# Delta recurrence: the second head of each pair contracts on the other 64 partitions, with exchanged copies of its k and qk products

## The chip, the cores and the metric

The kernel runs on one core of a Trainium2 chip. The metric is device time in microseconds (us); lower is better. Engines are named as the profile names them: PE (TensorE matmuls), PEld (TensorE weight loads), DVE (VectorE), ACT (ScalarE), POOL (GpSimd), SP (SyncE, which here issues most DMAs).

## The reference, cut to what matters

One decoder layer in fp32: a half-step feed-forward block, a combined projection, then two groups of eight heads side by side (dilated-window attention and a gated delta rule), an output projection, and a second half-step feed-forward block. 512 prompt tokens run beside 32 sample tokens (8 sequences of 4) that also read a key and value cache. The change touches the delta rule of the prompt. It goes in chunks of 64 tokens; the state `s` is 64x64 for each head and is carried from chunk to chunk:

```python
kd = k * exp(gc[..., -1:] - gc)               # k with decays
intra = tril(q @ k^T * decay)                # inside one chunk, 64x64 a head
...
def step(s, xs):
    v_new = u_i - w_i @ s
    o_i = qd_i @ s + intra_i @ v_new
    s = s * gl_i + kd_i^T @ v_new
    return s, o_i
```

So every chunk and head needs four products of 64x64 by 64x64: two with the state, then two with `v_new`. The last two, `kd_i^T @ v_new` and `intra_i @ v_new`, are the ones that the change makes in another way.

## The kernel before, in words

Dense products (both feed-forward blocks, the projections) are fp32 made of three passes over split operands, so each appears as `bank<-g,wh` twice and `bank<-g,wl` once. All of PE's products go through one helper and so bear one line, L309. One fp32 product of 64x64 shows as two MATMUL records of 64x64; a group of 16 records is 8 products.

The middle of the program (combined projection, delta rule, attention) is not written in the order in which it runs. It is written as lanes: Python generators that yield the engine, the planned microseconds and the PSUM banks of each next step. A planner, `Weave`, takes the step with the earliest planned start, and so sets the order of every engine's queue. A lane that needs buffers of the `g` pool yields ("G", n), and stands still until the planner's count of free slots allows it; ("G", -n) gives slots back. The pool has 63 buffers, of which the planner starts with `SLOTS - 23`. The lanes that matter here:

- `gemms()` makes the combined projection unit by unit (dense work, marked "PE*"); for the later units it asks for one slot before the first half of a unit. After light products the planner prefers dense ones that are ready.
- `weights()` casts the projection's weights on ACT (L921) and subtracts the high part on DVE (L923).
- `pair(j)` makes, for two heads (a pair, `hp` 0 and 1), the k-k and q-k products and writes IN[j] (the `intra` of both heads); `scale(j)` scales k to KD[j] on POOL; `inverse()` and `solve(j)` make the triangular inverse and the u and w operands. `solve` already uses two diagonal quarters of the PE array for pairs (`bank<-vu,wf`).
- `recurrence()` runs 8 steps, chunk after chunk. Step i = 2u + p2 has its 64 tokens on partitions r (the lower half where p2 is 0, the upper where it is 1); `ro` is the other half. One step: 16 products with the state (`bank<-state,wf` and `bank<-state,g`), a POOL multiply of the state (L1469), two DVE subtractions that make `v_new` in vv (L1474), 8 products into bank pk, KD with vv (L1481), and a DVE add that makes the new state (L1483).
- `chunk_out()`, one lane for each step, makes 8 products into bank pi, IN with vv (L1499), two DVE multiplies (L1502) and a DVE add of 64x512 (L1506). After each second step it makes the norm: an ACT square (L1511), a DVE reduction (L1514), some 13 small DVE operations (L1516 to L1520, helper lines 494 to 506), a POOL multiply (L1524), four PE transposes (L1529) and eight DVE multiplies (L1534).
- the attention's lanes: workers (L1731, L1746, L1812), the key cache (issued by SP at L1860, transposed by PE at L1866) and the value cache. The key loads need `g` slots; 15 of them come free when the recurrence ends.

In chunk_out and recurrence of before both heads of a pair read vv on the same partitions:

```python
mm(pk[64*hp:64*hp+64, j*64:j*64+64], KD[j][r, c0:c0+64], vv[r, j, hp])              # L1481
mm(pi[ro, (2*j+hp)*64:(2*j+hp)*64+64], IN[j][r, c0:c0+64], vv[r, j, hp])            # L1499
```

For pk the two heads of a pair use the same rows of the array (r) and different columns; for pi they use the same rows and the same columns (ro).

## Time and profile before

| | |
|---|---|
| median of the runs | 1219.39 us (3 runs, 1216.69 to 1222.22) |
| the profiled execution | 1218.54 us, of which the span is 1216.8 us |
| mean granted TensorE clock | 0.977 of full speed |
| PE busy | 1167.1 us, 96% of the span |
| DVE / ACT / POOL busy | 905.4 / 515.8 / 288.0 us |
| the eight recurrence steps | 600 to 667 us |

A row of the timeline gives the start, the length, the engine, the line and the form of a run of like instructions; ends of PE rows are modelled and overlap the next row, so the pitch from one row's start to the next is the better measure of what a group costs PE. In square brackets stands the idle time before a row and what ended it. Granted clock 1.00 is 2.4 GHz, the half of it is 1.2 GHz.

### The profile page before, as it was taken

How to read it: one execution, taken by the hardware profiler on the slowest of the kernel's cores; microseconds unless marked ns; L12 is line 12 of the kernel's file. 1: busy time of each engine (PE TensorE's matmuls, PEld its weight loads, DVE VectorE, ACT ScalarE, POOL GpSimd, SP SyncE). 2: the span in 40 equal slices, each digit the busy share in tenths (PEclk: the TensorE clock that was granted, in tenths of full speed). 3: DMA queues.
4: the chain of work that ended last, by engine and by line, in shares of the span. 5: the costliest groups of instructions: out<-in, count | busy, mean ns of one | idle time of the engine just before them, and what ended most of it. 6: DMA issues, size and time to landing. Idle time of an engine off the chain costs nothing.

```text
span 1216.8 us, 25657 instructions
## 1 busy us (share of the span) xinstructions
PE 1167.1 (96%) x10375; PEld 1104.9 (91%) x10375; DVE 905.4 (74%) x1905; ACT 515.8 (42%) x1035; POOL 288.0 (24%) x363
## 2 busy tenths in 40 slices
PE   8899999999999999999999999988999999999994
PEld 7899999999999888999888675877999999999994
DVE  6878887877766587794366647688988777777767
ACT  6444444343444465433411544456444444444432
POOL 2321121111100047961314100033211111111003
PEclk8999999999999999999999999989999999999997
DMA  7553323322233222336104995321322324242112
GB/s 169 152 174 97 115 88 108 105 73 87 70 97 121 75 69 78 97 91 159 58 13 124 322 299 191 114 77 46 113 92 73 98 79 122 87 122 70 56 50 74
DMA packets 165442, 130.91 MB, mean 108 GB/s; under 512 B 31758, under 2 KB 152100, under 8 KB 165324
## 3 DMA queue, kind: packets, MB, share of 16 engines
q1 hardware_dynamic: 163852, 124.82, 34.3%
q0 software_dynamic: 1472, 4.46, 1.2%
q8 instruction: 81, 1.33, 0.5%
q14 instruction: 37, 0.30, 0.1%
HBM read 119.63 MB, written 12.33 MB: 108 GB/s over the span
## 4 chain that ended last, share of the span: by engine, by line
PE 77%; DVE 10%; DMA 4%; POOL 3%; ACT 2%; SPq 2%; issue 2%; DVEq 0%; POOLq 0%; ACTq 0%
PE bank L309 73%; PE bank L525 1%; PE bank L1866 1%; DVE wl L313 1%; DMA wf<-in_ffn_w_gate 1%; DMA wf<-in_ffn_w_up 1%; DMA g<-in_cache_attn_k 1%; PE bank L582 1%; DVE wf L1333 1%; PE bank L1812 1%; DVE tmp L1331 1%; DVE wl L923 1%; DVE lna L504 1%; DVE g L313 1%; DVE g L1001 1%
## 5 line engine op out<-in xcount | busy, mean ns | idle before, releaser
L309 PE MATMUL bank<-g,wh 128*128 128x272 f32 (+2 forms) x4864 | 943.5, 292 | 11.9 <-DVE g L313 7.0
L309 PEld LDWEIGHTS bank<-g,wh 128*128 128x128 f32 x4864 | 769.4, 190 | 24.5 <-DVE g L313 7.6
L309 PE MATMUL bank<-g,wl 128*128 128x272 f32 (+2 forms) x2432 | 703.6, 290 | 0.0
L309 PEld LDWEIGHTS bank<-g,wl 128*128 128x128 f32 x2432 | 460.8, 190 | 3.6 <-issue 3.2
L312 ACT CAST wh<-wf 128x512 fp32r<-128x512 f32 (+2 forms) x176 | 111.7, 648 | 138.8 <-PE bank L309 113.0
L712 POOL TENSOR_TENSOR wf<-wf 128x512 f32<-128x512 f32 x40 | 63.7, 1592 | 360.5 <-DVE vu L710 344.9
L313 DVE TENSOR_TENSOR wl<-wf,wh 128x512 fp32r<-128x512 f32 (+2 forms) x172 | 135.6, 799 | 11.1 <-ACT wh L312 9.0
L309 PE MATMUL bank<-g 64*64 64x64 f32 (+15 forms) x1708 | 128.7, 295 | 3.7 <-DVE g L1596 2.4
L309 PEld LDWEIGHTS bank<-g 64*64 64x64 f32 (+7 forms) x1708 | 89.8, 142 | 23.2 <-issue 10.7
L312 ACT CAST wh<-vu 128x512 fp32r<-128x512 f32 x120 | 72.3, 618 | 70.7 <-PE bank L309 70.0
L713 POOL TENSOR_TENSOR vu<-wf,vu 128x512 f32<-128x512 f32 x40 | 59.7, 1493 | 125.4 <-DVE wl L313 121.1
L313 DVE TENSOR_TENSOR wl<-vu,wh 128x512 fp32r<-128x512 f32 x120 | 81.5, 693 | 10.4 <-ACT wh L312 6.2
L313 DVE TENSOR_TENSOR g<-g 128x544 fp32r<-128x544 f32 (+1 forms) x80 | 71.4, 919 | 0.0
L312 ACT CAST wh<-g 128x512 fp32r<-128x512 f32 x64 | 38.0, 618 | 59.5 <-issue 42.0
L312 ACT CAST g<-g 128x544 fp32r<-128x544 f32 (+1 forms) x80 | 44.3, 582 | 39.6 <-DVE g L755 24.0
L313 DVE TENSOR_TENSOR wl<-g,wh 128x512 fp32r<-128x512 f32 x64 | 43.0, 693 | 24.2 <-ACT wh L312 23.4
L887 ACT COPY g<-bank 128x512 f32<-128x512 f32 (+4 forms) x64 | 30.3, 501 | 60.0 <-PE bank L309 21.6
L923 DVE TENSOR_TENSOR wl<-wf,wh 128x1024 fp32r<-128x1024 f32 x28 | 37.7, 1348 | 20.6 <-ACT wh L921 20.4
L775 DVE TENSOR_TENSOR g<-bank,g 128x272 f32<-128x272 f32 x96 | 40.0, 431 | 12.5 <-PE bank L309 12.4
L711 DVE TENSOR_TENSOR vu<-vu,wf 128x512 f32<-128x512 f32 x40 | 47.6, 1190 | 1.8
L710 DVE TENSOR_TENSOR vu<-wf 128x512 f32<-128x512 f32 x40 | 27.5, 689 | 20.9 <-DMA wf<-in_ffn_w_gate 18.3
L921 ACT CAST wh<-wf 128x1024 fp32r<-128x1024 f32 x28 | 29.2, 1050 | 28.0 <-PE bank L309 14.0
(313 smaller groups left out, 1116.7 us busy)
## 6 DMA issues: line engine op xcount, KB each, us to landing
wf<-in_ffn_w_gate SPq DMA_DIRECT2D x21, 1024.0 KB
wf<-in_ffn_w_up SPq DMA_DIRECT2D x21, 1024.0 KB
g<-in_ffn_w_down SPq DMA_DIRECT2D x64, 256.0 KB
wf<-in_w_in SPq DMA_DIRECT2D x14, 1024.0 KB
g<-in_cache_attn_k SPq DMA_DIRECT2D x32, 256.0 KB
g<-in_cache_attn_v SPq DMA_DIRECT2D x32, 256.0 KB
wf<-in_ffn_w_down SPq DMA_DIRECT2D x8, 768.0 KB
wf<-in_w_out SPq DMA_DIRECT2D x4, 1024.0 KB
```

The lines of the kernel that those rows point to most:

```text
L309: return PE.matmul(out, l, r, start=start, stop=stop, skip_group_check=again)
L312: S.copy(h, f)
L313: (GP if pool else V).tensor_tensor(l, f, h.bitcast(F32), op=ALU.subtract)
L504: V.tensor_mul(a, y, y)
L710: V.tensor_add(s1, a21, a22)
L711: V.tensor_sub(s2, s1, a11)
L712: GP.tensor_tensor(a21, a11, a21, op=ALU.subtract)
L713: GP.tensor_tensor(s4, a12, s2, op=ALU.subtract)
L775: V.tensor_add(r, pd, r)
L887: return S.copy(out, src)
L921: S.copy(h, fm)
L923: V.tensor_sub(l, fm, h.bitcast(F32))
```

## The change

For the second head of each pair (hp 1), vv is written to the other half of the partitions (ro), and its KD and IN are read from copies in which the two halves of the partitions are exchanged (KX, IX). So the two heads of a pair contract on different rows of the array. `exchange()` makes the copies on ACT: two instructions of 64x256 for each of four pairs and each of KD and IN, 16 in all. They live in four more `g` buffers, taken one by one in `pair` (before its DMAs are issued) and at the end of `scale`, and given back when the recurrence ends (-19 where -15 was). The products into pi now land on ro for hp 0 and on r for hp 1, so the final add (one 64x512) becomes two of 64x256. The planned PE time of the pk and pi steps goes from 0.7 to 0.45, that of the add from 0.65 to 0.75.

```diff
@@ -1200,6 +1200,23 @@
         yield "G", -1
 
     EM, SD = {}, {}
+    KX, IX = {}, {}
+    def exchange(to, j, src):
+        if j % 2 == 0:
+            to[j // 2] = G(512)
+        x = to[j // 2][:, j % 2 * 256:j % 2 * 256 + 256].rearrange("p (u c) -> p u c", u=4)
+        for p2 in range(2):
+            S.copy(x[64 - 64 * p2:128 - 64 * p2], v4(src)[64 * p2:64 * p2 + 64, :, 1])
+
+    def chunk_of(own, exchanged, j, hp, u, p2):
+        if hp:
+            return exchanged[j // 2][64 - 64 * p2:128 - 64 * p2, j % 2 * 256 + u * 64:j % 2 * 256 + u * 64 + 64]
+        return own[j][64 * p2:64 * p2 + 64, u * 128:u * 128 + 64]
     A21 = [G(512) for _ in range(2)]
     svd = dp.tile([2, 2, 4, 4, 2, 32, 32], F32, name="svd")
     xd = dp.tile([2, 2, 4, 4, 2, 32, 32], F32, name="xd")
@@ -1260,6 +1277,10 @@
             yield "DVE", 0.35, [pa[hp]]
             V.tensor_tensor(v4(it)[:, :, hp], pv[hp][:, 1], v4(em)[:, :, hp], op=ALU.mult)
         IN[j] = it
+        if j % 2 == 0:
+            yield "G", 1
+        yield "ACT", 0.6
+        exchange(IX, j, it)
         av = at.rearrange("p (n c) -> p n c", n=8)
         for p2 in range(2):
             for hf in range(2):
@@ -1311,6 +1332,10 @@
             yield "POOL", 1.05
             x = VU[:, j] if c == 8 else a[j]
             GP.tensor_tensor(v4(x if out is None else out[j]), v4(x), b64(b[:, :, hs]), op=ALU.mult)
+        if j % 2 == 0:
+            yield "G", 1
+        yield "ACT", 0.6
+        exchange(KX, j, KD[j])
         wv.post(("scaled", j))
 
     def inverse():
@@ -1471,14 +1496,13 @@
                 vv = vn.rearrange("p (j t e) -> p j t e", j=4, t=2)
                 yield "DVE", 0.7
                 for hp in range(2):
-                    V.tensor_tensor(vv[r, :, hp], VU[r, :, u * 128 + hp * 64:u * 128 + hp * 64 + 64], pb[hp][r, :256].rearrange("p (j e) -> p j e", j=4),
+                    V.tensor_tensor(vv[(r, ro)[hp], :, hp], VU[r, :, u * 128 + hp * 64:u * 128 + hp * 64 + 64], pb[hp][r, :256].rearrange("p (j e) -> p j e", j=4),
                                     op=ALU.subtract)
-                yield "PE", 0.7, 2
+                yield "PE", 0.45, 2
                 pk, pi = wv.bank(), wv.bank()
                 for j in range(4):
                     for hp in range(2):
-                        c0 = u * 128 + hp * 64
-                        mm(pk[64 * hp:64 * hp + 64, j * 64:j * 64 + 64], KD[j][r, c0:c0 + 64], vv[r, j, hp])
+                        mm(pk[64 * hp:64 * hp + 64, j * 64:j * 64 + 64], chunk_of(KD, KX, j, hp, u, p2), vv[(r, ro)[hp], j, hp])
                 yield "DVE", 0.35, [pk]
                 V.tensor_tensor(sn, pk[:, :256].rearrange("p (j e) -> p j e", j=4), sn, op=ALU.add)
                 ST = sn
@@ -1486,24 +1510,25 @@
         for hp in range(2):
             GP.dma_start(sg_p[0, 0].rearrange("(j t) d e -> t d j e", t=2)[hp], ST[64 * hp:64 * hp + 64])
         yield "T", 6.0
-        yield "G", -15
+        yield "G", -19
 
     def chunk_out(u, p2, vv, pb, pi, ov):
         r = slice(64 * p2, 64 * p2 + 64)
         ro = slice(64 - 64 * p2, 128 - 64 * p2)
         ou = ov.rearrange("p j t e -> p (j t e)")
-        yield "PE", 0.7
+        yield "PE", 0.45
         for j in range(4):
             for hp in range(2):
-                c0 = u * 128 + hp * 64
-                mm(pi[ro, (2 * j + hp) * 64:(2 * j + hp) * 64 + 64], IN[j][r, c0:c0 + 64], vv[r, j, hp])
+                mm(pi[(ro, r)[hp], (2 * j + hp) * 64:(2 * j + hp) * 64 + 64], chunk_of(IN, IX, j, hp, u, p2), vv[(r, ro)[hp], j, hp])
         for hp in range(2):
             yield "DVE", 0.35, [pb[hp]]
             V.tensor_tensor(ov[ro, :, hp], pb[hp][ro, :256].rearrange("p (j e) -> p j e", j=4),
                             egs[ro, u, :].rearrange("p (j t) -> p j t", t=2)[:, :, hp, None].to_broadcast([64, 4, 64]),
                             op=ALU.mult)
-        yield "DVE", 0.65, [pi]
-        V.tensor_tensor(ou[ro], pi[ro], ou[ro], op=ALU.add)
+        yield "DVE", 0.75, [pi]
+        pv = pi.rearrange("p (j t e) -> p j t e", j=4, t=2)
+        for hp in range(2):
+            V.tensor_tensor(ov[ro, :, hp], pv[(ro, r)[hp], :, hp], ov[ro, :, hp], op=ALU.add)
         if p2 == 0:
             return
         yield "ACT", 0.55
```

The planner works out every engine's order from the planned times and the free slots, so the four more slots and the new planned times move work that the diff does not name. Three places:

PE of before, in the fifth recurrence step: the state products, dense products (`g,wh`, `g,wl`) that the planner put behind them, and then one group of eight products with vv.

```order
L309 MATMUL bank<-state,wf_7088 64x64 x4
L309 MATMUL bank<-state,g 64x64 x2
L309 MATMUL bank<-state,wf_7088 64x64 x4
L309 MATMUL bank<-state,g 64x64 x6
L309 MATMUL bank<-g,wh 128x256 x2
L309 MATMUL bank<-g,wl 128x256
L309 MATMUL bank<-g,wh 128x256 x2
L309 MATMUL bank<-g,wl 128x256
L309 MATMUL bank<-g 64x64 x16
```

PE of the changed kernel, the fifth and sixth steps, from the group with vv of the step before; L1554 are the transposes of the norm (L1529 before).

```order
L309 MATMUL bank<-g 64x64 x16
L309 MATMUL bank<-state,wf_7117 64x64 x8
L309 MATMUL bank<-state,g 64x64 x8
L309 MATMUL bank<-g 64x64 x16
L309 MATMUL bank<-state,wf_7117 64x64 x8
L309 MATMUL bank<-state,g 64x64 x8
L309 MATMUL bank<-g 64x64 x16
L1554 MATMUL bank<-cst,g 128x128 x4
L309 MATMUL bank<-g 64x64 x16
L309 MATMUL bank<-g,wh 128x256 x2
L309 MATMUL bank<-g,wl 128x256
```

The dense products that stood between the state products and the products with vv are gone from these two steps; from the fifth step to the eighth 24 dense matmuls stand where 110 stood, and the rest comes behind the recurrence, beside the first key transposes (L1866 before, L1891 now).

DVE of before, from the end of the fourth step into the fifth: small operations of a norm, the multiplies L1534 of the norm before, the subtractions L1474, the multiplies L1502, an evacuation (L888) and the new state (L1483).

```order
L505 SCALAR_TENSOR_TENSOR da<-da,oss 128x8
L1534 TENSOR_TENSOR g<-bank,g 128x64 x8
L506 SCALAR_TENSOR_TENSOR dy<-da,dy 128x8
L1474 TENSOR_TENSOR g<-vu,bank 64x4x64 x2
L1502 TENSOR_TENSOR g<-bank,egs 64x4x64 x2
L504 TENSOR_TENSOR da<-dy 128x8
L888 COPY g<-bank 128x512
L505 SCALAR_TENSOR_TENSOR da<-da,oss 128x8
L1483 TENSOR_TENSOR state<-bank,state 128x256
L506 SCALAR_TENSOR_TENSOR orr<-da,dy 128x8
L1506 TENSOR_TENSOR g<-bank,g 64x512
```

DVE of the changed kernel at the same place; L1499, L1525, L1507, L1531, L1539 and L1559 are L1474, L1502, L1483, L1506, L1514 and L1534 of before.

```order
L1499 TENSOR_TENSOR g<-vu,bank 64x4x64
L1525 TENSOR_TENSOR g<-bank,egs 64x4x64
L1499 TENSOR_TENSOR g<-vu,bank 64x4x64
L1525 TENSOR_TENSOR g<-bank,egs 64x4x64
L1559 TENSOR_TENSOR g<-bank,g 128x64 x8
L1507 TENSOR_TENSOR state<-bank,state 128x256
L1531 TENSOR_TENSOR g<-bank,g 64x4x64 x2
L1539 TENSOR_REDUCE oss<-g 128x8
L1499 TENSOR_TENSOR g<-vu,bank 64x4x64 x2
L1525 TENSOR_TENSOR g<-bank,egs 64x4x64 x2
L1541 TENSOR_TENSOR oss<-oss,rq_4909 128x8
L1542 TENSOR_SCALAR oss<-oss 128x8
```

Each add of chunk_out is two instructions now, and the eight multiplies of the norm and its reduction stand between one state and the next subtraction.

ACT of before, in the stretch that prepares the pairs: weight casts (L921), evacuations of the projection (L989, L991), squares (L1225, L1283) and the convolution's activation (L998).

```order
L921 CAST wh<-wf_5654 128x1024
L1225 ACTIVATE g<-g 128x512
L989 COPY g<-bank 128x256
L991 COPY g<-bank 128x32
L998 ACTIVATE g<-g,cw 128x512
L989 COPY g<-bank 128x256
L1283 ACTIVATE g<-g 128x512
L989 COPY g<-bank 128x256
L991 COPY g<-bank 128x32
```

ACT of the changed kernel at the same place, with the exchanging copies (L1213).

```order
L921 CAST wh<-wf_5654 128x1024
L989 COPY g<-bank 128x256
L991 COPY g<-bank 128x32
L1242 ACTIVATE g<-g 128x512
L1213 COPY g<-g 64x256 x2
L998 ACTIVATE g<-g,cw 128x512
L1213 COPY g<-g 64x256 x4
L989 COPY g<-bank 128x256
L1213 COPY g<-g 64x256 x2
L989 COPY g<-bank 128x256
```

Eight of the sixteen copies stand between the evacuations of the projection here.

## Rows read from the trace of the kernel before

**Rows 1.** Chain that ended last, 540 to 700 us: start us, us, what.
```profile
611.58 17.91 PE bank L309 x259
629.49 0.58 PE bank L1529 x4
...
671.48 9.05 DMA g<-in_cache_attn_k
```

**Rows 2.** Windows: stretch, length; busy us by engine (instructions); PE clock, DMA share, GB/s.
```profile
600.00:668.00 68.00, 67.45 (x936) 60.97 (x938) 44.70 (x152) 11.94 (x24) 25.48 (x48) 1.00 0.24 70
668.00:690.00 22.00, 19.52 (x148) 14.21 (x141) 14.40 (x51) 14.31 (x30) 4.02 (x7) 0.92 0.95 291
...
675.00:680.00 5.00, 3.10 (x28) 2.15 (x20) 3.62 (x18) 3.42 (x6) 0.00 (x0) 1.00 1.08 347
680.00:685.00 5.00, 4.42 (x28) 4.11 (x32) 4.23 (x11) 5.00 (x15) 0.56 (x1) 0.66 1.03 287
```

**Rows 3.** PE's waits, 440 to 860 us: waited for, us in total, times, longest.
```profile
PE bank L1866 <- DMA g<-in_cache_attn_k: 2.5, 2, 1.7
...
PE bank L1015 <- ACT g L1005: 2.0, 2, 1.1
```

**Rows 4.** PE timeline: eight products into pi (L1499), and dense rows behind.
```profile
606.66 1.14 PE L309 MATMUL bank<-g 64*64 64x64 f32 x16
607.74 0.50 PE L309 MATMUL bank<-g,wh 128*128 128x256 f32 x2
608.08 0.28 PE L309 MATMUL bank<-g,wl 128*128 128x256 f32 x1
...
608.43 0.28 PE L309 MATMUL bank<-g,wl 128*128 128x256 f32 x1
```

**Rows 5.** PE timeline: eight products into pk (L1481), and the row behind.
```profile
620.86 0.68 PE L309 MATMUL bank<-g 64*64 64x64 f32 x16
621.47 0.50 PE L309 MATMUL bank<-g,wh 128*128 128x256 f32 x2
```

**Rows 6.** PE timeline: 16 products on two diagonal quarters (solve), and the row behind.
```profile
577.50 1.15 PE L309 MATMUL bank<-vu,wf 64*64 64x64 f32 x32
578.58 0.50 PE L309 MATMUL bank<-g,wh 128*128 128x256 f32 x2
```

**Rows 7.** PE timeline: a step's 16 state products begin; the row behind the last.
```profile
600.35 0.51 PE L309 MATMUL bank<-state,wf 64*64 64x64 f32 x10
...
601.26 0.53 PE L309 MATMUL bank<-g,wh 128*128 128x288 f32 x2
```

**Rows 8.** Groups of 600 to 668 us: busy us, mean ns; idle before, releaser.
```profile
L1502 DVE TENSOR_TENSOR g<-bank,egs 64x256 f32<-64x256 f32 x16 | 6.5, 421 | 0.4
L1474 DVE TENSOR_TENSOR g<-vu,bank 64x256 f32<-64x256 f32 x16 | 6.3, 414 | 6.6 <-PE bank L309 6.4
...
L1506 DVE TENSOR_TENSOR g<-bank,g 64x512 f32<-64x512 f32 x8 | 5.5, 687 | 8.9 <-PE bank L309 8.8
...
L1731 DVE TENSOR_TENSOR g<-bank,g 128x128 f32<-128x128 f32 x16 | 3.7, 283 | 0.2
L1534 DVE TENSOR_TENSOR g<-bank,g 128x64 f32<-128x64 f32 x24 | 3.4, 212 | 2.8 <-PE bank L1529 2.8
L1483 DVE TENSOR_TENSOR state<-bank,state 128x256 f32<-128x256 f32 x8 | 3.3, 416 | 0.4 <-PE bank L309 0.3
```

**Rows 9.** DVE timeline: two of the norm's small operations.
```profile
638.76 0.17 DVE L504 TENSOR_TENSOR da<-dy 128x8 f32<-128x8 f32 x1
638.96 0.17 DVE L505 SCALAR_TENSOR_TENSOR da<-da,oss 128x8 f32<-128x8 f32 x1
```

**Rows 10.** Groups by form, 300 to 900 us, ACT: a copy of 256 columns.
```profile
L887 ACT COPY g<-bank 128x256 f32<-128x256 f32 x14 | 5.1, 373 | 24.1 <-PE bank L309 18.9 <-PE bank L1812 5.2
```

**Rows 11.** DVE timeline: the low half of a weight is made.
```profile
485.71 1.22 DVE L923 TENSOR_TENSOR wl<-wf,wh 128x1024 fp32r<-128x1024 f32 x1
```

**Rows 12.** PE timeline: the first product with that low half.
```profile
505.41 0.28 PE L309 MATMUL bank<-g,wl 128*128 128x256 f32 x1
```

## The prediction

> **What bounds the kernel now.** I read the table first: PE is busy in 96% of the span, so what is saved or added on PE counts in full, and what the other engines do counts only where PE waits for it. Then the windows around the recurrence [rows 2]: from 600 to 668 us PE is busy in 67.45 of 68 us at a granted clock of 1.00, while DVE has 44.70 us of work and ACT 11.94. The chain that ended last says the same: its long pieces there are PE's own products (259 of them in one piece of 17.91 us), and the first long piece that is not PE's is the wait for the first keys at 671.48 [rows 1]. So in the recurrence the dense products hide the chain state, subtraction, product, new state: whenever that chain has to wait for DVE, PE does a piece of the projection. This cover is the thing to watch, because the change takes slots and the planner orders by slots. Behind the recurrence PE is not quite full: 19.52 of 22 us from 668 to 690, at a clock of 0.92, with the DMA engines 95% busy [rows 2]; two waits there for the key load are 2.5 us [rows 3].
>
> **The change part by part.**
>
> A, the products. Eight products into pi (same rows and same columns of the array) take the pitch from 606.66 to 607.74, 1.08 us [rows 4]. Eight into pk (same rows, alternating columns) take 620.86 to 621.47, 0.61 us [rows 5]. The changed form has the two heads of a pair on different rows and different columns, writing one bank; the nearest row is solve's diagonal form, also into one bank, where 16 products take 577.50 to 578.58, 1.08 us, or 0.54 for eight [rows 6]. The gain for a chunk is (1.08 - 0.54) + (0.61 - 0.54) = 0.61, for eight chunks 4.9 us, all on PE, which sets the end: -4.9. Its bounds: if the pairs don't overlap at all, each eight takes 1.08, and A is 8 x (0.61 - 1.08) the wrong way, +3.8.
>
> A rule speaks against this form. In this trace the diagonal form writes one bank and still runs at half the price of the form on one tile [rows 4, 6]. The Trainium skill (TensorEngine Tiling (Array Packing), Restrictions and Gotchas) says that different row tiles cannot access the same PSUM bank at the same time; by it A would be +3.8 and not -4.9, but the solve row disagrees with it, so it stays a small rival. The same skill (TensorE: Matmul & The Clock Gate, Part 3, The mechanism) says that a weight load overlaps running products only where the row groups differ; by it pk would have cost 1.08 before and A would be -8.6, and the 0.61 of pk [rows 5] disagrees.
>
> B, the order. Four more slots are held until the recurrence ends, and the projection's lane, which wants one slot, stands still in the planner for most of steps 5 to 8. The order shows the result: steps 5 and 6 stand back to back on PE with no dense product between, and up to the end of step 8 only 24 dense matmuls stand where 110 stood. So there the chain through DVE is no longer covered. DVE's work from the subtractions of step 5 to the new state of step 8: each step has two subtractions (0.83), two multiplies (0.84), the two halves of the add (0.83, by the 64x256 rows) and the new state (0.42), 2.92, and four of them 11.7; two norms have a reduction (0.69, taken as the add of 512 columns), some 13 small operations at a pitch of 0.20 [rows 9] and eight multiplies of 0.212, 5.0 each, 10.0 for two; four of the workers' adds 1.1 more, less 1.4 of norm work that falls behind the last state: about 21.4 us [rows 8, 9]. PE's work in the same stretch: four times state products (0.91, from 600.35 to 601.26 [rows 7]) and twice 0.54, 8.0; eight dense threes at 0.35 (608.08 to 608.43 [rows 4]), 2.8; two groups of transposes at 0.58 [rows 1], 1.2; small products of other lanes about 1.5: 13.5 us. The difference, 7.9, is time in which PE has nothing: +8. The low end is what steps 5 and 6 alone give, where there is no dense product: DVE from the subtractions of step 5 to the new state of step 6 (subtractions and multiplies 1.67, L1534's eight 1.7, new state 0.42, adds 0.83, reduction 0.69, the next step's 1.67, four small ones 0.8, new state 0.42: 8.2) less PE's 4.6, about +4. The high end adds the delay from one engine to the next, some 2 us over eight handovers by the 0.2 us pitch of dependent small operations: +10. In before this cost nothing, since the dense products hid it.
>
> C, what is late next. The some 86 dense matmuls (10 us at 0.35 for three [rows 4]) that leave the recurrence come behind it, in the stretch where PE waited 2.5 us for keys [rows 3], and where after a stretch with 3.10 us busy of 5 the clock was granted at 0.66 for the next 5 [rows 2]. They fill these waits, and with the clock kept up the 4.42 busy us at 0.66 would be about 2.9, 1.5 less. The recurrence also ends earlier in PE's queue, so its slots come free earlier and the key loads start earlier. I take -4 (2.5 + 1.5), between 0 (DMA is then the limit all the same, at a share of 0.95 to 1.08) and -7 (the whole difference from full use over 668 to 690, 2.5, plus the clock's 1.5, plus 3 for keys that come sooner, a third of the 9.05 us piece [rows 1]).
>
> D, the adds. Eight adds of 0.687 become sixteen of about 0.416: 8 x (0.83 - 0.69) = 1.2 us more DVE work. In the first four steps DVE has gaps (8.8 us of idle ahead of these adds while it waits for PE [rows 8]), so nothing; in the last four it is in B already.
>
> E, the copies. Sixteen ACT copies of 64x256; the trace has none with 64 partitions, the nearest is 128x256 at 0.373 [rows 10], so 6.0 us of ACT work, between the evacuations and weight casts of 470 to 530 us. What covers them: a weight's low half is finished at 486.93 and first used at 505.41, 18 us later [rows 11, 12]. Each copy also waits for its source (POOL for KD, DVE for IN), and what is queued behind it on ACT, evacuations and the activation of the convolution, waits with it; PE waits for an activation of that stretch twice today, 2.0 us [rows 3]. I take 0, with an upper bound of +2, that wait doubled, and a lower bound of 0, since nothing is taken from ACT.
> In `pair` the copies of IN stand ahead of the four DMAs on SP and the POOL copies of A21, so each pair's blocks set off some 0.8 us later (two copies); the inverse waits for the last pair, and has dense work beside it.
>
> The sum against the profiled 1218.54 us: -4.9 + 8 - 4 + 0 + 0 = -0.9, so 1217.6, and against a median that is 0.85 above the profiled time 1218.5. I forecast 1218.
>
> **The rivals.**
>
> Faster: what PE loses in steps 5 to 8 comes back wholly, because the recurrence ends some 10 us earlier in PE's queue and the full DMA stretch behind it begins by so much earlier. B's net is 0: 1218.54 - 4.9 - 4 = 1209.6. For it speaks that the DMA engines stand nearly idle before 668 (share 0.24) and full behind [rows 2], so an earlier start has room; against it, that DVE's 21.4 us are added up from rows and stand in one queue.
>
> Slower: the clock. In steps 5 to 8 PE would be busy 13.5 of 21.4 us; before the fall to 0.66 at 680 it had been busy 3.10 of 5 [rows 2]. If the clock goes to 1.2 GHz in the compact steps, their 13.5 us of PE work become up to 27; some of it lies in DVE's time, but state products and products with v_new lie in the chain (8.0 us, doubled +8). It decides as soon as the clock falls within step 6: 1217.6 + 8 = 1226. Against it speaks that the dense products stand close on both sides.
>
> Not what it says: the pairs don't run side by side, as the page's rule has it. A is +3.8: 1217.6 + 8.7 = 1226. Against it stands the solve row [rows 6].
>
> A delay on ACT alone (E at +2) stays within the forecast: 1220.
>
> **How the numbers follow.** My forecast (A, B and C as sized, 1212.5 to 1224.6) has 0.53; the faster rival 0.22; the clock 0.20; no overlap 0.05. A measurement of this kernel can tell about 0.5%, 6.1 us, from no change: faster is below 1213.3, slower above 1225.5. Faster by more: the rival's 0.22 and 0.01 of my own range, 0.23. Slower by more: 0.20 + 0.05, less 0.02 for part of it under the bound, and 0.01 from my own range: 0.24. The same: 0.53. The range runs from just under the faster rival, 1209, to the clock rival with 2 us of E, 1228; out of it lie A without any of B (below) and clock and overlap together (above).
>
> **What would show it.** In the changed profile: groups of eight at a pitch of 0.54 for pi and for pk (A); PE idle of 4 to 10 us between the end of step 4 and the end of step 8, put down to DVE L1499 and L1507, with DVE near full there (B); the window around the first keys without the 2.5 us of waits and with a clock near 1.00 (C); no new wait for ACT between 470 and 530 (E). I am wrong if PE stays full in steps 5 to 8 (then the faster rival), if the clock there is under 0.9 (the slower), or if pi stays at 1.08.

## The result, and the profile after

The changed kernel takes 1225.97 us (median of 9 runs, 1223.68 to 1231.38), the kernel before 1219.39 us (9 runs as well). The ratio is 1.0059, 95% interval [1.0043, 1.0075]: slower by some 7 us, where 1218 us and no change were forecast. The time lies inside the range of 1209 to 1228, but a slower kernel is not what was forecast.

The profiled execution of the changed kernel took 1224.23 us, its span is 1222.3 us (before 1218.54 and 1216.8). I cut both traces at the same three points: the first state product of the recurrence, the start of the last new state, and the first instruction L574 (the norm behind the output projection). The windows of before between these points come first, then those of after; columns as in [rows 2].

```profile
600.35:664.66 64.31, 64.23 (x910) 58.08 (x909) 41.21 (x142) 10.27 (x21) 24.12 (x46) 1.00 0.22 63
664.66:807.46 142.80, 133.14 (x1100) 101.12 (x1100) 96.35 (x317) 63.84 (x160) 15.31 (x20) 0.96 0.64 203
```

```profile
601.52:658.05 56.53, 51.65 (x821) 46.07 (x821) 44.80 (x152) 8.66 (x17) 18.73 (x25) 0.91 0.14 43
658.05:813.53 155.48, 143.60 (x1205) 110.44 (x1199) 99.85 (x327) 64.39 (x161) 24.11 (x44) 0.98 0.64 198
```

In before PE is never without work in the recurrence (64.23 of 64.31 us); in after it is busy 51.65 of 56.53 us, at a clock of 0.91. The recurrence is 7.8 us shorter, but it holds fewer dense matmuls. The groups of that stretch show how many, first before, then after (busy us, mean ns):

```profile
L309 PE MATMUL bank<-g,wh 128*128 128x256 f32 (+1 forms) x152 | 31.7, 301 | 0.0
L309 PE MATMUL bank<-g,wl 128*128 128x256 f32 (+1 forms) x77 | 22.6, 293 | 0.0
```

```profile
L309 PE MATMUL bank<-g,wh 128*128 128x288 f32 (+1 forms) x100 | 21.8, 309 | 0.0
L309 PE MATMUL bank<-g,wl 128*128 128x288 f32 (+1 forms) x51 | 14.8, 290 | 0.0
```

That is 229 before and 151 after: 78 dense matmuls left, at 0.35 us for three [rows 4] about 9.1 us (an estimate from that row). With it the ledger of the two spans is: up to the first state product 601.52 - 600.35 = +1.2; the recurrence 56.53 + 9.1 - 64.31 = +1.3; behind it, up to L574, 155.48 - 9.1 - 142.80 = +3.6; the rest of the span (408.77 against 409.34) -0.6. The sum is +5.5, which is the difference of the spans.

This ledger counts dense matmuls alone, but transposes have moved too: those of the keys (L1866) out of the recurrence, where the changed kernel has none, and those of the values (L964) into it. In the same stretch, two rows of before and one of after:

```profile
L1866 PE MATMUL bank<-cst,g 128*128 128x128 f32 x16 | 2.4, 283 | 0.0
L964 PE MATMUL bank<-cst,g 128*128 128x128 f32 x12 | 1.9, 282 | 0.0
```

```profile
L964 PE MATMUL bank<-cst,g 128*128 128x128 f32 x20 | 3.1, 275 | 0.0
```

So 2.4 us of transposes have gone behind the recurrence, and 1.2 us have come into it from ahead. With them the ledger is about +2.4 ahead of the recurrence, +2.5 in it, +1.2 behind it and -0.6 after that. These are single profiles: before, e1, e5, e9, e10 and e11 have one and the same order up to the first state product, and it stands anywhere from 598.11 (e9) to 600.35 us (before). So a difference of some 2 us in one stretch may be scatter.

PE's timeline in after shows the uncovered steps: what ends each wait stands in the brackets.

```profile
631.95 0.51 PE L309 MATMUL bank<-state,wf 64*64 64x64 f32 x10 [0.44 <-DVE state L1507]
634.76 2.04 PE L309 MATMUL bank<-g 64*64 64x64 f32 x32 [1.84 <-DVE g L1499]
637.37 0.80 PE L309 MATMUL bank<-state,wf 64*64 64x64 f32 x10 [0.56 <-DVE da L504]
641.68 0.69 PE L1554 MATMUL bank<-cst,g 128*128 128x128 f32 x2 [0.80 <-POOL g L1549]
```

The windows of 4 us around them show the clock that followed:

```profile
628.00:632.00 4.00, 3.56 (x53) 3.26 (x52) 2.54 (x13) 0.41 (x1) 0.03 (x1) 1.00 0.00 0
632.00:636.00 4.00, 2.04 (x55) 1.77 (x58) 2.93 (x8) 0.63 (x1) 0.58 (x1) 0.88 0.02 4
636.00:640.00 4.00, 3.44 (x71) 3.16 (x66) 3.57 (x15) 0.00 (x0) 0.61 (x1) 0.50 0.00 0
640.00:644.00 4.00, 3.20 (x46) 2.68 (x44) 3.81 (x19) 0.00 (x0) 1.04 (x1) 0.50 0.01 4
```

PE waits 1.84 us for the subtraction L1499, is busy 2.04 of 4 us, and from 636 to 644 its granted clock is 0.50, that is 1.2 GHz, while DVE is busy 3.57 and 3.81 of 4 us. Both things that the prediction held apart, DVE's queue and the clock, happened here one after the other. Over all of steps 5 to 8 PE is idle for 4.35 of 26.05 us, its granted clock is 0.80, and DVE is busy 22.08 us:

```profile
632.00:658.05 26.05, 21.70 (x367) 19.15 (x368) 22.08 (x84) 2.79 (x7) 6.89 (x10) 0.80 0.18 49
```

The products themselves are nearly as cheap as forecast. PE's timeline in after, a group of 16 products (pk and pi one behind the other) and a single group of eight, each with the row behind it:

```profile
607.74 0.68 PE L309 MATMUL bank<-g 64*64 64x64 f32 x16
608.35 0.50 PE L309 MATMUL bank<-g,wh 128*128 128x256 f32 x2
...
615.01 1.20 PE L309 MATMUL bank<-g 64*64 64x64 f32 x32
616.13 0.53 PE L309 MATMUL bank<-g,wh 128*128 128x288 f32 x2
```

Sixteen take 1.12 us and eight alone 0.61, where eight into pi took 1.08 [rows 4].

Behind the recurrence the keys come later, although the recurrence ends 6.6 us earlier on the clock of the trace. SP's issues of the first key loads, before and then after:

```profile
637.15 25.26 SPq L1860 DMA_DIRECT2D g<-in_cache_attn_k  x8
```

```profile
658.34 17.44 SPq L1885 DMA_DIRECT2D g<-in_cache_attn_k  x8
```

In before the first key loads are issued during the recurrence; in after SP issues its first at 658.34, while the last new state is made (from 658.05). PE's waits from 440 to 860 us in after, to be read beside [rows 3]:

```profile
PE bank L1015 <- ACT g L1005: 5.6, 3, 4.1
...
PE bank L1992 <- DVE g L1989: 2.5, 1, 2.5
PE bank L309 <- DVE sm L1821: 2.4, 2, 2.1
PE bank L582 <- DVE g L574: 2.4, 1, 2.4
PE bank L309 <- DVE g L1499: 1.8, 1, 1.8
PE bank L1891 <- DMA g<-in_cache_attn_k: 1.6, 1, 1.6
PE bank L1554 <- POOL g L1549: 1.4, 2, 0.8
```

The wait for keys is 1.6 us where it was 2.5, but waits for DVE in the attention have come (L1821 in a worker, L1989 in the samples' part), and PE's idle time behind the recurrence is 155.48 - 143.60 = 11.9 us against 142.80 - 133.14 = 9.7.

### The profile page after: what moved, and what is told of

It is laid out like the page before. It is cut to its first block, busy times and chain, and to the rows that moved or that the text cites. A ratio compares the mean times of both kernels' runs of the same rounds, so it can differ in the third digit from the quotient of the medians.

```text
span 1222.3 us, 25682 instructions
## 1 busy us (share of the span) xinstructions
PE 1164.1 (95%) x10375; PEld 1101.8 (90%) x10375; DVE 908.1 (74%) x1921; ACT 517.1 (42%) x1043; POOL 286.5 (23%) x363
## 4 chain that ended last, share of the span: by engine, by line
PE 74%; DVE 12%; DMA 6%; POOL 3%; ACT 2%; issue 2%; SPq 1%; DVEq 0%; POOLq 0%; ACTq 0%
PE bank L309 70%; DVE wl L313 2%; DMA wf<-in_w_in 1%; DVE g L313 1%; DMA wf<-in_w_out 1%; PE bank L525 1%; PE bank L1891 1%; DMA wf<-in_ffn_w_gate 1%; DVE wl L923 1%; DMA wf<-in_ffn_w_up 1%; PE bank L582 1%; PE bank L1837 1%; DMA brep<-bvec 1%; DVE vu L711 1%; DMA g<-in_x_prompt 1%
## 5 line engine op out<-in xcount | busy, mean ns | idle before, releaser
L309 PE MATMUL bank<-g 64*64 64x64 f32 (+16 forms) x1708 | 123.3, 298 | 9.1 <-DVE g L1621 2.8
L309 PEld LDWEIGHTS bank<-g 64*64 64x64 f32 (+7 forms) x1708 | 83.8, 143 | 27.1 <-issue 9.9
L313 DVE TENSOR_TENSOR g<-g 128x544 fp32r<-128x544 f32 (+1 forms) x80 | 68.9, 888 | 0.0
L887 ACT COPY g<-bank 128x512 f32<-128x512 f32 (+5 forms) x57 | 27.4, 499 | 50.7 <-PE bank L1891 18.7
L921 ACT CAST wh<-wf 128x1024 fp32r<-128x1024 f32 x28 | 29.3, 1049 | 46.1 <-DMA wf<-in_w_in 26.1
```

The source lines that it names most:

```text
L309: return PE.matmul(out, l, r, start=start, stop=stop, skip_group_check=again)
L313: (GP if pool else V).tensor_tensor(l, f, h.bitcast(F32), op=ALU.subtract)
L887: return S.copy(out, src)
L921: S.copy(h, fm)
```

## The experiments

The theory to test: the products give their gain, and the loss comes from the order, the steps that lost their cover and what follows behind them. Rivals: the products of the second row group cost something elsewhere; the 16 copies in ACT's queue make the loss; the new planned times make an order of their own, whatever the slots. All ratios are against the kernel before.

### The products alone (e1)

```diff
-    V.tensor_tensor(vv[r, :, hp], VU[r, ...
+    V.tensor_tensor(vv[(r, ro)[hp], :, hp], VU[r, ...
...
-    mm(pk[...], KD[j][r, c0:c0 + 64], vv[r, j, hp])
+    mm(pk[...], KD[j][(r, ro)[hp], c0:c0 + 64], vv[(r, ro)[hp], j, hp])
...
-    mm(pi[ro, ...], IN[j][r, c0:c0 + 64], vv[r, j, hp])
+    mm(pi[(ro, r)[hp], ...], IN[j][(r, ro)[hp], c0:c0 + 64], vv[(r, ro)[hp], j, hp])
...                              # and the add in two instructions, as in the change
```

> The kernel before with the products of the change alone: a pair's second head contracts on the other half of the partitions and the add is two instructions, but there are no copies and no held slots, and the planned times are the old ones. The exchanged copies are left out, so the second heads multiply the wrong half of KD and IN; the work on PE is the same. If the products give what the changed trace shows (16 products at a pitch of 1.12 us where pk and pi took 0.61 + 1.08), the gain is 8 x 0.57 = 4.6 us: 1214.8 us, ratio 0.996. If the second row group or the shared bank costs what it saves elsewhere (the two adds, the exchanged vv), 1219 to 1223, ratio 1.000 to 1.003.

Measured: 0.9975 [0.9960, 0.9990], 3 us faster. Windows of the recurrence and behind it:

```profile
599.03:660.45 61.42, 60.74 (x910) 54.72 (x909) 43.31 (x150) 10.40 (x21) 24.10 (x46) 1.00 0.22 66
660.45:801.61 141.16, 131.65 (x1100) 99.94 (x1100) 95.94 (x319) 63.65 (x160) 15.29 (x20) 0.98 0.64 206
```

With the order of before (the same 152 and 77 dense records in the recurrence) it is 61.42 us where it was 64.31: -2.9. The products give their gain when the cover stays; the term A was of the right sign and about 2 us too large.

### The order without the copies (e2), the copies without the products (e3)

e2 is the changed kernel without the two calls of `exchange`; the planned steps and the held slots stay:

```diff
         yield "ACT", 0.6
-        exchange(IX, j, it)
...
         yield "ACT", 0.6
-        exchange(KX, j, KD[j])
...
-            return exchanged[j // 2][64 - 64 * p2:128 - 64 * p2, ...]
+            return own[j][64 - 64 * p2:128 - 64 * p2, u * 128 + 64:u * 128 + 128]
```

> The changed kernel in its own order, with the four slots held, but without the 16 ACT copies (the exchange is left out; the second heads multiply the wrong half of KD and IN). If the copies' place in ACT's queue (PE's 4.10 us wait for the activation L1005 at 486 and the half clock behind it) is part of the loss, this is 2 to 4 us under the changed kernel: 1222 to 1224, ratio 1.002 to 1.004. If the loss is the order alone, 1226, ratio 1.006.

Measured: 1.0103 [1.0081, 1.0126]. Without the copies the kernel is not faster than with them; it is slower, outside both expectations. The wait of PE for L1005 is there without them too:

```profile
PE bank L1015 <- ACT g L1005: 4.0, 2, 3.5
```

But e2 does not run in the changed kernel's order, as the expectation took for granted. Where the changed kernel's PE has 64 records of 64x64 in one piece (first row), e2 has them in two, with dense products between, and DVE's and ACT's orders differ around there too:

```profile
478.20 1.30 PE L309 MATMUL bank<-g 64*64 64x64 f32 x64
```

```profile
475.49 1.20 PE L309 MATMUL bank<-g 64*64 64x64 f32 x32
484.14 2.03 PE L309 MATMUL bank<-g 64*64 64x64 f32 x32
```

So e2 does not price the copies. Its first state product stands at 599.11, 2.4 us ahead of the changed kernel's 601.52, which is hardly more than the scatter of that point; behind the recurrence e2 takes 159.01 us where the changed kernel takes 155.48. That the copies are not what makes the loss is shown better by e4 and e12 below, which make all sixteen and lose 1.4 and 2.3 parts in a thousand. Why e2 loses more than the changed kernel, the runs do not show.

e3 makes the copies and holds the slots, and leaves the products, the add and the planned times as they were.

> The kernel before with the 16 copies and the four held slots, but with the products, the add and the planned times of before: the copies are not read. If the held slots and copies make the loss, it is 1219.4 plus the loss of the changed kernel (6.6) plus what the products had given back: 1228 to 1231, ratio 1.007 to 1.010. If instead the new products or their planned times make the loss, it is 1219 to 1221, ratio 1.000 to 1.001.

Measured: 1.0094 [1.0073, 1.0115]. Copies and held slots, with the products of before, lose more than the whole change. The kernel that differs from e3 in the products and adds alone is e12 below, at 1.0023: there the products give most of the loss back, 8.6 us, where in the order of before they gained 3 (e1). In e3's profile PE is busy 57.91 of 63.28 us in the recurrence, at a clock of 0.89: the uncovered steps again, without any of the new products. The rival that the new products make the loss falls with e1 and e3.

### More slots for the planner (e4, e8)

The pool keeps its 63 buffers; only the planner's count changes (e4 -19, e8 -21).

```diff
-    wv = Weave({a + b: 1 for a in "AB" for b in "0123"}, BK, SLOTS - 23)
+    wv = Weave({a + b: 1 for a in "AB" for b in "0123"}, BK, SLOTS - 19)
```

> The changed kernel, but the planner starts with four more slots (the pool keeps its 63 buffers): dense products stand between steps 5 to 8 again, 101 where the changed kernel has 24. If the lost cover makes the loss (4.8 us of PE idle from 628 to 656, and about 10 us at half clock that cost 4.9), this is 9 to 10 us under the changed kernel: 1216 to 1218, ratio 0.997 to 0.999. If the copies make it, 1225 to 1226, ratio 1.005.

> The changed kernel with two more planned slots where e4 had four: 89 dense matmuls between steps 5 and 8, the first key transposes behind the same dense product as in e4. If the cover is what counts, the ratio is 0.998 to 1.002, like e4; if the order behind the recurrence decides as much, it may come out anywhere up to 1.006, although the cover is there.

Measured: e4 1.0014 [0.9998, 1.0029], e8 1.0034 [1.0018, 1.0050], the changed kernel 1.0059. The windows of e4:

```profile
599.25:658.27 59.02, 57.68 (x886) 52.42 (x886) 43.77 (x151) 8.13 (x17) 21.60 (x43) 1.00 0.18 47
658.27:809.28 151.01, 135.68 (x1130) 102.73 (x1129) 93.87 (x317) 69.38 (x173) 17.67 (x21) 0.96 0.64 202
```

With 241 dense records in the recurrence the cover is back: PE's idle time there is 1.3 us (4.9 in the changed kernel) and the clock stays at 1.00. With 90 dense matmuls more than in the changed kernel (10.5 us at the same pitch) it takes only 2.5 us longer: the cover is worth about 8 us there, or 6 when the 14 transposes that it has less (about 2 us) are counted too, and B was +8. But the total gains only 5 us, half of what I expected, because the stretch behind is not 9.1 us shorter with 78 dense matmuls gone from it (the other 12 come from ahead of the recurrence), but 4.5: PE is idle for 15.3 us in it. e8 shows the same: 0.8 us idle in the recurrence (60.80 busy of 61.56), 16.4 behind it (132.44 of 148.87). The cover can be had back and still be lost behind.

### Other columns, no copies (e5)

```diff
-    mm(pi[ro, (2*j+hp)*64:(2*j+hp)*64+64], IN[j][r, c0:c0+64], vv[r, j, hp])
+    mm(pi[(ro, r)[hp], (2*j+hp)*64:(2*j+hp)*64+64], IN[j][r, c0:c0+64], vv[r, j, hp])
...
-    V.tensor_tensor(ou[ro], pi[ro], ou[ro], op=ALU.add)
+    pv = pi.rearrange("p (j t e) -> p j t e", j=4, t=2)
+    for hp in range(2):
+        V.tensor_tensor(ov[ro, :, hp], pv[(ro, r)[hp], :, hp], ov[ro, :, hp], op=ALU.add)
```

> The kernel before with one thing of the change: the second head's products into pi go to the other half of pi's partitions, so that a pair alternates columns as pk's always did, with the same rows; no copies, no held slots, the add in two instructions, planned times of before. If alternating columns alone give pi the 0.61 that pk had, the gain is 8 x (1.08 - 0.61) = 3.8 us: ratio 0.997, and nearly all that the products of the change gave (ratio 0.9975) needs no copies. If the gain needs other rows, it is 0 to 1 us slower by the adds: 1.000 to 1.001.

Measured: 0.9970 [0.9953, 0.9987]. Its group of eight into pi, and the row behind it:

```profile
606.01 0.68 PE L309 MATMUL bank<-g 64*64 64x64 f32 x16
606.62 0.51 PE L309 MATMUL bank<-g,wh 128*128 128x256 f32 x2
```

0.61 us, the same as in the changed kernel and as pk always had [rows 5]. e1, with other rows besides, runs in the same order as e5, and their recurrences take 61.42 and 61.31 us. The whole gain of the products comes from the columns of pi; the other rows, and with them the copies and the slots, add nothing that these traces show. This kernel does what the change meant to do and is 3.7 us faster than before.

### Late copies (e6)

The copies are made, and the slots taken, by a lane of their own, for which the recurrence waits:

```diff
+    def exchanges():
+        for j in range(4):
+            yield "wait", ("scaled", j)
+            yield "wait", ("pair", j)
+        yield "wait", ("solved", 0)
+        for j in range(4):
+            if j % 2 == 0:
+                yield "G", 2
+            yield "ACT", 0.6
+            exchange(IX, j, IN[j])
+            yield "ACT", 0.6
+            exchange(KX, j, KD[j])
+        wv.post("exchanged")
```

> The changed kernel with the 16 copies made, and the four slots taken, only when the first pair is solved (about 575 us); the planner's slots are as before. The planner's order then keeps 86 dense matmuls between steps 5 and 8 (the changed kernel 24). If the lost cover and what follows from it make the loss, the ratio is 0.997 to 1.001; if the loss comes from the copies or from holding slots at all, 1.004 to 1.006.

Measured: 1.0018 [1.0003, 1.0033]. This lies between the two expectations, nearer the first: all the copies and all four slots, and 5 us less loss than with early copies, only from when the copies are made and the slots taken. In its profile the recurrence has 2.3 us idle (53.94 busy of 56.23) and the part behind 13.0 (134.95 of 147.98): as in e4, the cover is mostly back and the part behind has got worse.

### Planned times (e11, e12)

e11 is e5 with the planned times of the change; e12 is the changed kernel with the planned times of before.

```diff
-        yield "PE", 0.7
+        yield "PE", 0.45
...
-        yield "DVE", 0.65, [pi]
+        yield "DVE", 0.75, [pi]
```

> e5 with the planned times of the change (0.45 for pi, 0.75 for the add): no copies and no held slots, but the planner puts 66 dense matmuls between steps 5 and 8 where e5 has 108, and none between the last two. If cover is what counts, about a third of what the changed kernel lost there comes in: 0.999 to 1.001 against e5's 0.997. If the planned times are harmless, 0.996 to 0.998.

> The changed kernel with the planned times of before (0.7, 0.7, 0.65): the four slots are held and steps 5 to 7 stand back to back again (30 dense matmuls up to step 8, where the changed kernel has 24). If the held slots make the order, it is no better than the changed kernel: 1.004 to 1.008. If the planned times made it, 0.998 to 1.002.

Measured: e11 1.0023 [1.0006, 1.0039], e12 1.0023 [1.0007, 1.0040]. Two numbers of the plan alone turn e5's gain into a small loss, 6 us, more than I expected. e11's two windows are

```profile
599.96:656.88 56.92, 55.39 (x856) 49.08 (x857) 40.21 (x138) 8.85 (x17) 23.15 (x45) 1.00 0.17 48
656.88:804.86 147.98, 134.14 (x1148) 103.09 (x1146) 98.91 (x334) 64.14 (x163) 16.47 (x22) 0.98 0.66 204
```

with 1.5 us idle in the recurrence and 13.8 behind it (e5: 0.4 and 9.7). This profile is of a run 3.3 us under e11's median, so it holds only 2 of the 6 us, most of them behind the recurrence. e12 is the other way round: 3.6 us idle in the recurrence at a clock of 0.88 (55.26 busy of 58.90), and 9.0 behind:

```profile
658.80:807.73 148.93, 139.92 (x1179) 107.49 (x1173) 97.15 (x315) 67.43 (x167) 15.52 (x21) 0.98 0.65 208
```

It disagrees with the first of its expectations and stands just above the second. All copies, the held slots and the uncovered steps are there, and still it loses 4.4 us less than the changed kernel. So the new planned times are a cause of their own, of about the same size without the slots (e5 to e11, 5.3 parts in a thousand) and with them (e12 to the changed kernel, 3.6). Much of what they cost the changed kernel lies behind the recurrence: there e12 has 460 dense matmuls, 52 more than before, about 6.1 us, so that by the first ledger it stands at 148.93 - 6.1 - 142.80 = 0.0 where the changed kernel stands at +3.6. Its keys are no reason, for seven of the first eight are issued as late as there:

```profile
646.85 0.37 SPq L1885 DMA_DIRECT2D g<-in_cache_attn_k  x1
658.39 1.47 SPq L1885 DMA_DIRECT2D g<-in_cache_attn_k  x3
660.45 8.67 SPq L1885 DMA_DIRECT2D g<-in_cache_attn_k  x4
```

### When the keys come (e7, e9, e10, e15)

The first eight key loads wait in the plan until more slots are free, 8 in e7, e9 and e10, 6 in e15. e7 and e15 have it on top of e4, e9 on the kernel before, e10 on e5.

```diff
         for g, j, b in todo:
-            yield "G", 2
+            if (g, j) < (0, 2):
+                yield "G", 8
+                yield "G", -6
+            else:
+                yield "G", 2
```

> The kernel of four more planned slots (ratio 1.0014), but each of the first eight key loads waits in the plan until 8 slots are free, not 2; the order of the recurrence stays the same. If keys that come later are a cost of their own behind the recurrence, this is 2 to 5 us slower than that kernel: ratio 1.003 to 1.0055. If only the cover in the recurrence counts, 1.000 to 1.002.

> e7 with a threshold of 6 free slots in place of 8 for the first eight key loads; the recurrence's order is the same as in e4 and e7. If later keys help an order that is covered, it lies between e4 (1.0014) and e7 (0.9933): 0.995 to 1.000. If e7 was one lucky arrangement, anything from 0.993 to 1.004.

> The kernel before with one edit: each of the first eight key loads waits in the plan until 8 slots are free, as in e7; products, copies and slots as before. If later keys are a gain of their own, which has nothing to do with the change, the ratio is 0.993 to 0.997. If they only repair what the order of e4 had spoilt behind the recurrence, 0.999 to 1.002.

> e5 (pi on alternating columns, no copies) with the same key edit. If both gains add up: e5's 0.997 less 0.3 to 0.7%, ratio 0.990 to 0.994. If the key edit only repairs e4's order: 0.996 to 0.998.

Measured: e7 0.9933 [0.9909, 0.9957], e15 0.9950 [0.9936, 0.9964], e9 1.0060 [1.0041, 1.0078], e10 1.0031 [1.0017, 1.0044]. In e4's order later keys are a gain of 0.6 to 0.8%, against both expectations for e7; in the order of before and of e5 the same edit loses 0.6%, against all four for e9 and e10. The windows of e7:

```profile
600.88:659.93 59.05, 57.73 (x897) 52.54 (x897) 43.39 (x150) 8.52 (x18) 21.52 (x43) 1.00 0.20 53
659.93:802.53 142.60, 134.91 (x1113) 102.17 (x1108) 92.41 (x316) 65.29 (x166) 13.04 (x19) 0.95 0.67 207
```

The recurrence is that of e4 to 0.1 us; behind it PE's idle time fell from 15.3 to 7.7 us, and its waits for key loads, 4.9 us in e4, are gone. So e4's loss behind is idle time which nearly the same work in another order does not have. e7 is the fastest kernel of this study, 8 us under the one before, and it contains the whole change. Its first key loads come nearly as late as the changed kernel's; e4's, then e7's:

```profile
640.66 18.52 SPq L1885 DMA_DIRECT2D g<-in_cache_attn_k  x7
```

```profile
656.67 2.07 SPq L1889 DMA_DIRECT2D g<-in_cache_attn_k  x2
```

e9 and e10 lose elsewhere than behind the recurrence, where they take 143.40 us (142.80 before) and 140.31 (141.34 in e5). In e9's profile 6.0 us come behind L574 (415.3 us against 409.3). In e10's the recurrence takes 69.63 us for 61.31 in e5, with 24 dense matmuls more (2.8 us), at a clock of 0.88: from about 629 to 646 us the granted clock was 0.50, and before it fell PE had been busy without a gap.

```profile
620.00:625.00 5.00, 5.00 (x77) 4.80 (x76) 4.56 (x19) 0.38 (x1) 1.64 (x2) 1.00 0.00 0
630.00:635.00 5.00, 5.00 (x54) 4.58 (x54) 1.66 (x4) 1.04 (x2) 0.00 (x0) 0.50 0.00 0
```

That profile is of e10's slowest run of twelve, so how much of e10's loss the clock is, it does not show.

### Uncovered steps with slots for the keys (e13, e14)

The planner has more slots, but the projection's lane may take one only while 5 (e13, on -19) or 3 (e14, on -21) are free.

```diff
             if n > 5 and hf == 0:
-                yield "G", 1
+                yield "G", 5
+                yield "G", -4
```

> Four more planned slots as in e4, but the projection's lane may take one only while 5 are free: steps 6 to 8 stand back to back as in the changed kernel (12 dense matmuls between steps 5 and 8; 24 there), while the key loads have the slots. If the gain forecast behind the recurrence failed because the keys came too late, this is 3 to 5 us under the changed kernel: ratio 1.001 to 1.003. If the uncovered steps are the loss whatever the keys do, it stays at 1.005 to 1.008.

> Two more planned slots, the projection's lane taking one only while 3 are free: 13 dense matmuls between steps 5 and 8, steps 5 to 7 back to back. The same two outcomes as for e13: 1.001 to 1.003 if late keys are the cause, 1.005 to 1.008 if the uncovered steps are.

Measured: e13 0.9994 [0.9981, 1.0007], e14 1.0054 [1.0036, 1.0072]. The part behind the recurrence, e13 and then e14:

```profile
652.72:808.43 155.71, 148.57 (x1208) 114.28 (x1205) 95.25 (x326) 64.47 (x165) 19.43 (x40) 0.95 0.64 197
```

```profile
656.78:809.10 152.32, 143.86 (x1199) 109.90 (x1193) 93.62 (x324) 66.54 (x167) 17.53 (x39) 0.98 0.65 203
```

and e13's first key loads:

```profile
653.00 20.12 SPq L1886 DMA_DIRECT2D g<-in_cache_attn_k  x14
```

e13 has uncovered steps (3.4 us idle in the recurrence, clock 0.94) and loses nothing: with the four slots it issues 14 key loads in 20.12 us from 653.00, where the changed kernel issued 8 in 17.44 us from 658.34, and PE is idle for 7.1 us behind, not 11.9. e14, with two more slots, issues 9 from 658.23, has 8.5 us idle behind and 5.5 in the recurrence, at a clock of 0.88, and stays a loss. e13 is better than both its expectations, e14 agrees with its second.

Does e13 show that the keys were the cause? Not so. Its stretch behind the recurrence holds as many instructions on PE as the changed kernel's (1208 and 1205; 487 and 486 dense matmuls) and takes as long, 155.71 us against 155.48: what it has less of idle time it loses at a clock of 0.95 for 0.98. In both kernels the first key load comes 0.3 us behind the start of the last new state. What e13 gains is there before: its last new state starts at 652.72, the changed kernel's at 658.05, with 11 dense matmuls (1.3 us) less ahead of it. So its gain lies in the order ahead of the recurrence and in it, which the edit changes too (the first state product comes at 591.56). That the displaced work fills the waits behind as soon as the keys have slots, these two runs do not show.

## Why the prediction was wrong, point by point

**A, the products: right, the size somewhat high.** -4.9 forecast. Two single groups take 1.08 + 0.61 before and 0.61 + 0.61 after, 8 x 0.47 = 3.8; e1 measures -3 us in all and -2.9 in the recurrence. What was too large is the 0.54 for eight: it is the half of sixteen in a row [rows 6], and sixteen in a row do take 1.12 here, but a single eight takes 0.61, so that pk gained nothing. The bound of +3.8 falls: the diagonal form does not cost what one tile costs. By the Trainium skill (TensorEngine Tiling (Array Packing), Restrictions and Gotchas) two row groups could not use one bank at the same time; the rows do not bear out the price that I drew from it, since eight products of two row groups into one bank take 0.61, not 1.08. By its other rule (TensorE: Matmul & The Clock Gate, Part 3, The mechanism) the weight loads would overlap only where the row groups differ; e5's pi has the same rows, other columns, and takes the same 0.61. What I had not asked is whether the rows were needed at all: pk's 0.61 [rows 5] was the row that said no.

**B, the order: right in place and sign, half right in kind.** +8 forecast, as idle time. A and B together were +3.1; the ledger of the recurrence gives +1.3, or +2.5 with the transposes, and with e1's -2.9 for A that leaves +4.2 to +5.4, the lower half of +4 to +10; by e4, which restores the cover, it is 6 to 8. It was not idle time alone. Of the 7.9 us of idle time in steps 5 to 8 there are 4.35, and beside them stands a clock of 0.80 over these steps, 0.50 from 636 to 644. I had named a clock under 0.9 there as the sign of the slower rival, and it came. But the fall was a part of B's time and not 8 us on top of it, so the rival was half right, and that B's size fits is in part luck. The other profiles agree: where PE is idle for more than 2 us in the recurrence (the changed kernel, e2, e3, e6, e12, e13, e14) the clock there is 0.88 to 0.97, elsewhere 1.00, but for e10.

**C, what is late next: the step that failed.** -4 forecast, +3.6 measured, or +1.2 with the transposes counted. It rested on two sentences. "They fill these waits": they did not. The stretch behind is 12.7 us longer for about 9.1 us of dense products and 2.4 us of transposes. The wait for keys did fall from 2.5 to 1.6 us, but other waits came behind it, for DVE in the attention, and the idle time rose from 9.7 to 11.9 us. "The key loads start earlier": they started 21 us later, 658.34 against 637.15. Before, they ran during the recurrence; with four slots more for the planner (e4) seven of them run there again, from 640.66. I had written down that the four slots are held until the end of the recurrence and had used it for the projection's lane only, not for the other lane that asks for slots.

But that the late keys are what C cost is not shown, and three kernels speak against it: e12, whose keys are as late but for one, is level behind the recurrence and 4.4 us faster in all; e7, with its first keys at 656.67, has 7.7 us idle there; e13, with more keys sooner, takes no less time there. What the runs do show is that the planned order decides whether displaced work finds waits to fill, and that the new planned times, which I had not looked at by themselves, are a part of the order that did not. The cause within that order stays open. Had I taken C at 0, the upper end that I gave it, the sum would have been 1221.6; with the +3.6 it is 1225.2, between the profiled 1224.23 and the median of 1225.97. That it comes so near is in part luck, since the other terms are off too: +1.3 for A and B where I had +3.1, and +1.2 ahead of the recurrence where I had 0.

**D and E.** D, the two adds, costs nothing that shows: e5 has them, and gains. E was bounded at 0 to +2, and its sign did show: PE waits 4.1 us for the activation L1005 in one piece, 5.6 us in all where it was 2.0, and 5.4 to 7.7 us in every profile with early copies, while the 2.2 us that PE of before waits for DVE's L1261 there are gone. Without the copies it is 4.0 us (e2), so at least a part is the new order, which I had not looked at ahead of the recurrence. What it cost in the end is not shown: the first state product comes 1.2 us later, with 1.2 us of transposes less ahead of it, about the upper bound and about the scatter of that point. The copies of 64x256 take 0.40 us each; the row of 0.373 [rows 10] was a fair one.

**The rivals.** "Faster", with B's net at 0, did not come: the stretch behind the recurrence began 6.6 us earlier and took 12.7 us longer. "Not what it says" fell with the row of 1.12. "Slower" had the right time, 1226, by a mechanism that is only a part of it. One bound of mine does not come out of its terms: -4.9 + 4 - 7 from 1219.39 is 1211.5, where I wrote 1212.5; nothing hangs on it.

What stays open: why the changed kernel's order leaves the waits behind the recurrence unfilled, why later keys help in e4's order (e7, e15) and hurt in the order of before (e9, e10), and why e2 loses more than the changed kernel. The part behind the recurrence takes between 140 and 159 us in these profiles, and with the same 408 dense matmuls 142.80 us before and 151.01 in e4; its idle time runs from 7 to 16 us. The runs show that the order decides it, and not by which rule.

## What to carry to other kernels

An exchange of partitions, a copy or a held buffer is paid in the buffers that other lanes then don't get: before pricing the instructions, list every lane that asks the same pool and where each would stand without its slot. A planned time that is corrected along with a change is a second change, to be run by itself (e11, e12): here it cost more than the products had gained. Where a planner sets the order, test the arithmetic alone in the old order (e1) and the new order without the arithmetic (e3) before believing a sum of both. And look first for the smallest form of the idea: other columns gave here what other rows were built for, with no copy and no slot (e5).

## What the runs showed of the hardware

Eight small fp32 products in pairs take as little time when the two of a pair share rows and differ in columns (0.61 us, e5) as when they differ in both (0.61, the changed kernel); on one tile they take 1.08 [rows 4]. An ACT copy of 64x256 in fp32 that moves data to the other half of the partitions takes 0.403 to 0.408 us in the trace, near the 0.373 of a 128x256 copy from a bank [rows 10]. PE's clock fell to 0.50 after waits of 0.44 and 1.84 us in the changed kernel, and in e10's recurrence with no wait before it.
